# A hybrid HGRN2 and retention layer: one tree for two heads and two blocks, and 512-column retention q/k products

## The chip, the cores and the metric

The kernel runs on one core of a Trainium2 chip. The metric is the device time of one execution in microseconds (us). The engines are named as the profile names them: PE (TensorE matmuls) and PEld (its weight loads), DVE (VectorE), ACT (ScalarE), POOL (GpSimd) and SP (SyncE, which here only issues DMAs; SPq is its queue of issues). Each engine takes its own instructions in a fixed order; an instruction that waits holds up all that stand behind it on that engine.

## The reference

One layer over 2048 positions with model width 1024 and 8 heads of each of two mixers:

```python
h    = rms_norm(x, norm_g) * (1.0 + scale) + shift
proj = h @ w_in
(hq, hf, hi, hz, rq, rk, rv, rz, ga, gb) = split(proj)
oA = hgrn2_chunkwise(hq, hf, hi, lower_bounds)     # S_t = diag(f_t) S_{t-1} + (1-f_t) i_t^T
uA = head_rms_norm(oA, hg_norm_g) * silu(hz)
qB, kB = rotary(rq, pos), rotary(rk, pos)
oB = retention_chunkwise(qB, kB, rv)               # chunks of 128, zeta/xi decays
uB = head_rms_norm(oB, ret_norm_g) * silu(rz)
m  = sigmoid(ga) * uA + sigmoid(gb) * uB
x  = x + gate * (m @ w_out)
out = rms_norm(x, final_g)
```

The HGRN2 heads have 128 channels for q, f and v, the retention heads 64 for q and k and 128 for v. All is float32; dense products are made as three float32r products of a high and a low part.

## The kernel before, in words

**Tiling.** The sequence is cut into two superblocks (sb) of 1024 tokens, each of 8 chunks of 128 or two blocks of 512. In a superblock four pairs of heads (p = 0 to 3) follow one another. For a pair, PE runs four dense stages: **a** (forget gate and q of HGRN2, `gf` and `gq`, four groups for each block), **c** (the v of both mixers, `gv`, one group a chunk), **b** (retention's q and k, `gr`, one group of 256 columns a chunk) and **d** (the gates of the two heads, `gg`, 8 chunks for each head). A group is 8 steps over the contraction (kt = 0 to 7) of three matmuls each (`mm3`), so 24 matmuls. All dense matmuls are recorded under L53.

**Weights.** `Ring` (L447) brings them in the order of use. SP loads a raw tile of two steps (`wa`, `wb`, `wc`, `wd`, L465/L467; two raw tiles exist, NRAW), ACT copies the high part of a step (L482), DVE subtracts for the low part (L483), and the split step sits in one of 9 slots. A slot is freed in the last group of a stage, step by step; a raw tile is free when both its steps are split.

**Background.** Between dense matmuls stand bursts of small ones. `Background.tick` counts dense steps (1 tick is one step of 512 columns) and after GAP = 8 ticks lets every lane give out its next piece: `tree` (seven levels of products `lv` for the HGRN2 scores inside a chunk, one tree for each block and pair of heads, two of them side by side), `retention` (`rt`, then `por`) and `hgrn_out` (`poh`, with the running state `st`). After level 64 a tree transposes k into f on DVE (L666) and posts `place`, 16 DMAs `k<-f` on SP (L673), after which `hgrn_out` may read k by tokens. `rotate` makes the rotary parts on DVE (L760 to L769), transposes them (L772) and posts `send`, four DMAs `qkT<-tr` to DRAM (L777). `fetch` in `retention` makes `kpad` with the decay zeta on DVE (L796) and posts three DMAs from DRAM (L805, L806) into `qpad` and `kT`. A post comes out a given number of ticks later.

**Order.** PE's order is that of the program. All DMAs stand in one queue, SP's. On SP, DVE, ACT and POOL the order is set by the scheduler of the compiler framework and fixed before the run. DVE's `v`, `st`, `qk`, `qs`, `tr`, `wl..` in the profile are the tiles named above.

Of the kernel before, what the change touches and what calls it, by code (L numbers as in the profile page):

```python
# [9 lines left out]
F32 = mybir.dt.float32  # L10
# [12 lines left out]
P = 128  # L23
# [12 lines left out]
NQK = 6  # L36
NGA = 6
GAP = 8.0
# [4 lines left out]
def tile_hybrid(ctx: ExitStack, tc: tile.TileContext, a: dict, out: bass.AP):  # L43
# [47 lines left out]
    def late_consts():  # L91
        m32 = upool.tile([P, 512], I32, name="m32", tag="sg", bufs=3)
        nc.sync.dma_start(out=m32[:, 0:66], in_=a["msk"])
        G.tensor_copy(
            out=msk, in_=m32[:, 0:64].rearrange("p (l t) -> p l t", l=4).unsqueeze(2).broadcast_to([P, 4, 8, 16])
        )
        G.tensor_copy(out=dmsk, in_=m32[:, 64:66].unsqueeze(1).broadcast_to([P, 8, 2]))
        for t, src in lates:
            nc.sync.dma_start(out=t, in_=src)
# [50 lines left out]
    def ada_row_of_c():  # L150

        scb = hpool.tile([P, D], F32, name="scb", tag="h1", bufs=8)
        for i in range(2):
            dg = upool.tile([P, 1025], F32, name=f"dg{i}", tag="k", bufs=2)[:, 0:512]
            for k4 in range(4):
                kt = 4 * i + k4
                V.tensor_scalar(
                    out=dg[:, k4 * P : (k4 + 1) * P], in0=ident, scalar1=sc[:, kt : kt + 1], scalar2=None, op0=ALU.mult
                )
            ps = dense_ps(f"scp{i}")  # L160
            PE.matmul(out=ps, lhsT=ones, rhs=dg, start=True, stop=True)
            V.tensor_copy(out=scb[:, i * 512 : (i + 1) * 512], in_=ps)
# [13 lines left out]
    def ada_row(j):  # L176

        acc = upool.tile([P, 1025], F32, name=f"acc{j}", tag="k", bufs=2)[:, 0:512]
        bg_ = upool.tile([P, 1024], F32, name=f"gate{j}", tag="q", bufs=2)[:, 0:512]
# [20 lines left out]
    msk = cpool.tile([P, 4, 8, 16], U8, name="msk", tag="msk")  # L200
    dmsk = cpool.tile([P, 8, 2], U8, name="dmsk", tag="dmsk")
# [4 lines left out]
    afs, ads = [], []  # L206
    for i in range(2):
        t = cpool.tile([P, 8, P], F32, name=f"af{i}", tag=f"af{i}")
        G.memset(t, 0.0)
        afs.append(t)  # L210
        t = cpool.tile([P, 8, 32], F32, name=f"ad{i}", tag=f"ad{i}")
        G.memset(t, 0.0)
        ads.append(t)
# [122 lines left out]
    def load_x2(t, nm, tag):  # L336
        xt = upool.tile([P, {"q": 1024, "f": 1026}[tag]], F32, name=f"{nm}{t}", tag=tag, bufs=2)[:, 0:1024]
# [50 lines left out]
    def block_r(b):  # L388

        while held.get("f", 0) > 1:  # L390
            yield True
        take("f", 2)
        rb = upool.tile([P, 2, 513], F32, name=f"rb{b}", tag="f", bufs=2)[:, 0, 0:512]
        for t in range(4):
            xt = upool.tile([P, 1024], F32, name=f"xt{b}_{t}", tag="xr", bufs=1)
            nc.sync.dma_start(out=xt, in_=a["x"][(4 * b + t) * P : (4 * b + t + 1) * P, :])
            yield
            yield
            r = x_rstd(t, [xt[:, 0:512], xt[:, 512:1024]], f"b{b}_{t}")
# [9 lines left out]
    def block_h(b):  # L409
# [9 lines left out]
        for kt in range(KT):  # L419
# [8 lines left out]
            else:  # L428
                if kt == KT - 1:
                    give("f")  # L430
# [4 lines left out]
    for sb in range(NSB):  # L435
        for p in range(NP):
            if sb == 0 and p == 0:
                wseq += [(("c", sb, p), a["w_c"][p], 512), (("a", sb, p), a["w_a"][p], 512)]
            else:
                wseq += [(("a", sb, p), a["w_a"][p], 512), (("c", sb, p), a["w_c"][p], 512)]  # L440
            wseq.append((("b", sb, p), a["w_b"][p], 256))
            wseq.append((("d", sb, 2 * p), a["w_d"][2 * p], 512))
            wseq.append((("d", sb, 2 * p + 1), a["w_d"][2 * p + 1], 512))


    slots = [(g, k, 512 // wseq[g][2]) for g in range(len(wseq)) for k in range(0, KT, 512 // wseq[g][2])]

    class Ring:
        def __init__(self):
            self.pairs = [(g, k2) for g in range(len(wseq)) for k2 in range(KT // 2)]  # L450
            self.raw_of = {gk: i for i, gk in enumerate(self.pairs)}
# [7 lines left out]
        def load(self, upto):  # L459
            while self.nraw < min(upto, len(self.pairs)):  # L460
                g, k2 = self.pairs[self.nraw]
                key, src, n = wseq[g]
                w = wpool.tile([P, 2, 512], F32, name=f"w{key[0]}{g}_{k2}", tag="raw", bufs=NRAW)
                if n == 512:
                    nc.sync.dma_start(out=w, in_=src[k2])  # L465
                else:
                    nc.sync.dma_start(out=w[:, 0, :].rearrange("p (k n) -> p k n", k=2), in_=src[k2])  # L467
# [3 lines left out]
        def pump(self, limit=RING):  # L471
            while self.nsplit < min(self.nfree + limit, len(slots)):
                i = self.nsplit
                g, k, two = slots[i]
                key, src, n = wseq[g]
                r = self.raw_of[g, k // 2]
                self.load(r + 1)
                w = self.raws[r].rearrange("p k n -> p (k n)")
                w = w[:, 0:512] if two == 2 else w[:, k % 2 * 512 : k % 2 * 512 + 512]
# [4 lines left out]
                for j in range(two):  # L484
                    self.tiles[key, k + j] = (hi[:, j * n : (j + 1) * n], lo[:, j * n : (j + 1) * n])
                self.nsplit += 1
                done = r + (two == 2 or k % 2 == 1)
                self.load(done + self.ahead)
# [12 lines left out]
    def group_tok(sb, key, cs, n, nm):  # L501

        pss = [dense_ps(f"{nm}_{sb * CH + c}") for c in cs]
        tok_steps(sb, key, cs, n, pss, range(KT))
        return pss

    def tok_steps(sb, key, cs, n, pss, kts):
        for kt in kts:
            ws = ring.tiles[key, kt]
            for c, ps in zip(cs, pss):  # L510
                hh = hts[sb * NBLK + c // 4, kt]
                t = c % 4
                done = mm3(
                    ps[:, 0:n],
                    (hh[0][:, t * P : (t + 1) * P], hh[1][:, t * P : (t + 1) * P]),
                    (ws[0][:, 0:n], ws[1][:, 0:n]),
                    kt == 0,
                    kt == KT - 1,
                )
            if cs[-1] == CH - 1 and (n == 512 or kt % 2):  # L520
                ring.release()
            bg.tick(n / 512 * len(cs))
        return done
# [19 lines left out]
    us = {}  # L543

# [5 lines left out]
    def unit_f(h, b, psf, f, k):  # L550
        j = h % 2
        sg = upool.tile([P, 512], F32, name=f"sgf{h}_{b}", tag="sg", bufs=3)
        S.activation(out=sg, in_=psf, func=AF.Sigmoid)
        if j == 0:
            V.memset(f[:, :, 512:513], 1.0)
        V.tensor_scalar(
            out=f[:, j, 0:512], in0=sg, scalar1=omlb[:, h : h + 1], scalar2=lb[:, h : h + 1], op0=ALU.mult, op1=ALU.add
        )
        V.tensor_scalar(
            out=k[:, j * 512 : (j + 1) * 512], in0=f[:, j, 0:512], scalar1=-1.0, scalar2=1.0, op0=ALU.mult, op1=ALU.add  # L560
        )

    def unit_q(h, b, psq, q):
        j = h % 2
        sg = upool.tile([P, 512], F32, name=f"sgq{h}_{b}", tag="sg", bufs=3)
        S.activation(out=sg, in_=psq, func=AF.Sigmoid)
        V.tensor_tensor(out=q[:, j * 512 : (j + 1) * 512], in0=psq, in1=sg, op=ALU.mult)

    level = {}

    def level_ps(i):

        if level.get("burst") != bg.bursts:
            level["burst"] = bg.bursts
            level["ps"] = small_ps(f"lv{bg.bursts}", "lv")
        return level["ps"][:, i * 256 : (i + 1) * 256]

    def tree(p, b, f, k, q):
        nm = f"{p}_{b}"
        af, ad = afs[b % 2], ads[b % 2]  # L580
        f0 = upool.tile([P, 2], F32, name=f"f0{nm}", tag="f0", bufs=4)
        V.tensor_copy(out=f0, in_=f[:, :, 0])
        kk = k[:, 0:1024]
        k16, q16 = (z.rearrange("p (n t) -> p n t", t=16) for z in (kk, q))
        k16j = kk.rearrange("p (j n t) -> p j n t", j=2, t=16)
        qk0 = upool.tile([P, 64], F32, name=f"qk0{nm}", tag="qk0", bufs=1)
# [6 lines left out]
        for li in range(7):  # L593
            m = 1 << li
            yield
            ps = level_ps(b % 2)
            qm, km = (z.rearrange("p (n two m) -> p n two m", two=2, m=m) for z in (q, kk))
            if m < 16:
                for c in range(8):
# [9 lines left out]
            else:  # L609
                nr = 64 // m  # L610
                for n in range(8 * nr):
# [6 lines left out]
            if m == 1:  # L618
                for u in range(4):
                    PE.matmul(  # L620
                        out=ps[32 * u : 32 * u + 32, 128:144], lhsT=ones[:, 0:32],
                        rhs=qk0.rearrange("p (c u w) -> p c u w", u=4, w=2)[:, :, u, :], start=True, stop=True,
                    )
            yield "mid"
            t_cur = f[:, :, 1:513] if m == 1 else f[:, :, 0 : 2 * nb]
            tv = t_cur.rearrange("p j (n two) -> p j n two", two=2)
            qv = q.rearrange("p (j n two m) -> p j n two m", j=2, two=2, m=m)[:, :, :, 1, :]
            kv = kk if m >= 16 else k[:, 1:1025]
            kv = kv.rearrange("p (j n two m) -> p j n two m", j=2, two=2, m=m)[:, :, :, 0, :]
            V.tensor_tensor(out=qv, in0=qv, in1=tv[:, :, :, 0:1].broadcast_to([P, 2, nb, m]), op=ALU.mult)  # L630
            V.tensor_tensor(out=kv, in0=kv, in1=tv[:, :, :, 1:2].broadcast_to([P, 2, nb, m]), op=ALU.mult)
# [4 lines left out]
            if m == 1:  # L636
                V.copy_predicated(
                    out=ad.rearrange("p c (w j) -> p c w j", w=2)[:, :, :, 0], mask=dmsk,
                    data=ps[:, 128:144].rearrange("p (c w) -> p c w", w=2),
                )  # L640
            if m < 16:
# [3 lines left out]
                    data=ps[:, 0:128].rearrange("p (n m) -> p n m", m=m),  # L645
                )
            elif m == 64:
                for u in range(2):
                    S.activation(
                        out=af[0:64, u : 8 : 2, 64:P],  # L650
                        in_=ps[64 * u : 64 * u + 64, 0:256].rearrange("p (c t) -> p c t", c=4), func=AF.Copy,
                    )
            else:
                for r0 in range(0, P, 2 * m):
                    S.activation(
                        out=af[r0 : r0 + m, :, r0 + m : r0 + 2 * m],
                        in_=ps[r0 : r0 + m, 0 : 8 * m].rearrange("p (c t) -> p c t", c=8), func=AF.Copy,
# [5 lines left out]
        tl = upool.tile([P, 8], F32, name=f"tl{nm}", tag="tl", bufs=4)  # L663
# [569 lines left out]
```

## Time and profile before

| what | number |
|---|---|
| median of three runs | 2119.55 us (2117.77 to 2121.07) |
| the profiled execution | 2116.81 us |
| its span in the trace | 2114.9 us |
| mean granted clock of PE | 0.996 |
| DVE, ACT, POOL busy | 54%, 28%, 6% |
| DMA | 171.05 MB, mean 81 GB/s |

The span runs from the first to the last instruction of the trace; 1.9 us of the profiled execution lie around it. In the chain of waits, and in groups of instructions, the first number of a row is the start or the total in us; in the timeline it is the start, then how long the row lasts, and in brackets how long the engine was idle before it and what it waited for.

### The profile page before, as it was taken

Reading aid. Unit: us, or ns where it says so; the run is one execution under the profiler, and the core shown is the slowest. Engines: PE = TensorE matmul, PEld = TensorE weight load, DVE = VectorE, ACT = ScalarE, POOL = GpSimd, SP = SyncE. Lnnn points to the kernel's source line nnn. Section 1 sums busy time; section 2 is a strip of 40 time slices with the busy share of each in tenths; the row PEclk is TensorE's granted clock in tenths of the full one; section 3 lists DMA queues with packets and bytes.
Section 4 is the critical chain, followed back from the end, with each engine's and each line's share of the span. In section 5 each row is a group of like instructions: output and inputs, shape, how many; then the busy total and the mean of one; then the engine's idle time right before and its main releaser. Section 6 shows DMA issues by size and latency. Waiting matters only on the chain.

```text
span 2114.9 us, 40661 instructions
## 1 busy us (share of the span) xinstructions
PE 2068.9 (98%) x16152; PEld 1747.7 (83%) x16152; DVE 1144.2 (54%) x2977; ACT 589.6 (28%) x1485; POOL 135.9 (6%) x276
## 2 busy tenths in 40 slices
PE   6998999999999999999999999999999999999998
PEld 4887888988888888987888888988888888877886
DVE  7385535654555444657655444653545545566553
ACT  6222213222222223234222223222222223223221
POOL 1001100110001000121001000110001000100000
PEclk9999999999999999999999999999999999999999
DMA  8132211422132211435132211421132212336541
GB/s 321 36 78 50 62 45 47 107 64 53 37 75 58 59 60 45 101 105 157 36 76 57 59 62 45 95 63 49 40 80 52 72 58 61 85 105 210 175 134 60
DMA packets 298365, 171.05 MB, mean 81 GB/s; under 512 B 222912, under 2 KB 259264, under 8 KB 298176
## 3 DMA queue, kind: packets, MB, share of 16 engines
q1 hardware_dynamic: 298176, 168.47, 28.6%
q8 instruction: 127, 2.08, 0.4%
q14 instruction: 62, 0.51, 0.1%
HBM read 134.81 MB, written 25.17 MB: 76 GB/s over the span
## 4 chain that ended last, share of the span: by engine, by line
PE 89%; DVE 4%; DMA 3%; SPq 2%; issue 1%; ACT 0%; POOL 0%; DVEq 0%; POOLq 0%; ACTq 0%
PE gg L53 32%; PE gv L53 15%; PE gq L53 8%; PE gf L53 8%; PE ops L53 8%; PE gr L53 5%; PE por L53 4%; PE lv L53 3%; PE poh L53 3%; PE rt L53 1%; SPq L777 1%; SPq L673 1%; DVE wa L169 1%; DMA wd<-in_w_d_dram 1%; DMA kT<-qkT 1%
## 5 line engine op out<-in xcount | busy, mean ns | idle before, releaser
L53 PE MATMUL gg<-whd,h 128*128 128x512 f32 x2048 | 656.8, 394 | 0.0
L53 PEld LDWEIGHTS gg<-whd,h 128*128 128x128 f32 x2048 | 385.9, 188 | 78.2 <-issue 0.5
L53 PE MATMUL gg<-wld,h 128*128 128x512 f32 x1024 | 399.8, 390 | 0.0
L53 PE MATMUL gv<-whc,h 128*128 128x512 f32 x1024 | 335.4, 399 | 0.0
L53 PEld LDWEIGHTS gv<-whc,h 128*128 128x128 f32 x1024 | 192.6, 189 | 42.0 <-DVE h L363 0.8
L53 PEld LDWEIGHTS gg<-wld,h 128*128 128x128 f32 x1024 | 193.2, 189 | 37.8 <-issue 0.5
L53 PE MATMUL gv<-wlc,h 128*128 128x512 f32 x512 | 199.1, 391 | 1.1 <-DVE wlc L483 1.1
L53 PE MATMUL gr<-whb,h 128*128 128x256 f32 x1024 | 192.2, 285 | 0.0
L855 ACT ACTIVATE sgg<-gg 128x512 f32<-128x512 f32 x128 | 76.1, 595 | 336.2 <-PE gg L53 329.2
L53 PEld LDWEIGHTS gr<-whb,h 128*128 128x128 f32 x1024 | 161.9, 191 | 0.4
L630 DVE TENSOR_TENSOR q<-q,f 128x512 f32<-128x512 f32 x112 | 77.1, 688 | 157.4 <-PE lv L53 157.1
L53 PE MATMUL gf<-h,wha 128*128 128x512 f32 x512 | 159.0, 392 | 1.4 <-ACT wha L482 1.3
L53 PE MATMUL gq<-h,wha 128*128 128x512 f32 x512 | 160.0, 394 | 0.0
L53 PE MATMUL ops<-wo,mh 128*128 128x512 f32 x512 | 157.7, 389 | 0.0
L858 DVE TENSOR_TENSOR ga<-gg,sgg 128x256 f32<-128x256 f32 x128 | 53.8, 420 | 180.5 <-ACT sgg L855 173.4
L53 PE MATMUL gr<-wlb,h 128*128 128x256 f32 x512 | 144.8, 283 | 0.0
L53 PEld LDWEIGHTS gv<-wlc,h 128*128 128x128 f32 x512 | 96.7, 189 | 20.1 <-DVE wlc L483 1.5
L53 PEld LDWEIGHTS gf<-h,wha 128*128 128x128 f32 x512 | 95.3, 188 | 21.6 <-ACT wha L482 2.2
L53 PEld LDWEIGHTS ops<-wo,mh 128*128 128x128 f32 x512 | 96.1, 188 | 19.9
L53 PEld LDWEIGHTS gq<-h,wha 128*128 128x128 f32 x512 | 94.8, 188 | 19.4
L53 PE MATMUL gf<-h,wla 128*128 128x512 f32 x256 | 100.3, 392 | 0.0
L53 PE MATMUL gq<-h,wla 128*128 128x512 f32 x256 | 99.9, 390 | 0.0
(157 smaller groups left out, 2924.8 us busy)
## 6 DMA issues: line engine op xcount, KB each, us to landing
wd<-in_w_d_dram SPq DMA_DIRECT2D x64, 512.0 KB, 3.8
wc<-in_w_c_dram SPq DMA_DIRECT2D x32, 512.0 KB, 3.4
wa<-in_w_a_dram SPq DMA_DIRECT2D x32, 512.0 KB, 3.6
wa<-in_w_ada_dram SPq DMA_DIRECT2D x16, 512.0 KB, 8.4
wb<-in_w_b_dram SPq DMA_DIRECT2D x32, 256.0 KB, 2.6
qkT<-tr SPq DMA_DIRECT2D x256, 32.0 KB, 1.7
k<-f SPq DMA_DIRECT2D x256, 32.0 KB, 2.0
mT_dram<-ga SPq DMA_DIRECT2D x512, 16.0 KB, 1.5
```

The source lines that it names most:

```text
L53: made = nc.tensor.matmul(**kw)
L169: V.tensor_tensor_reduce(out=w, in0=w, in1=scb, scale=1.0, scalar=bad[:, i * KT + kt : i * KT + kt + 1], op0=ALU.mult, op1=ALU.add, accum_ ...
L630: V.tensor_tensor(out=qv, in0=qv, in1=tv[:, :, :, 0:1].broadcast_to([P, 2, nb, m]), op=ALU.mult)
L673: nc.sync.dma_start(out=placed[32 * j : 32 * j + 32, :, i, :], in_=turned[32 * i : 32 * i + 32, :, j, :])
L777: nc.sync.dma_start(out=dm[:, 32 * i : 32 * i + 32].rearrange("(j a) t -> a j t", a=32), in_=tr[32 * i : 32 * i + 32].rearrange("a (j t) - ...
L855: S.activation(out=sg, in_=ps, func=AF.Sigmoid)
L858: V.tensor_tensor(out=ga, in0=ps[:, 0:256], in1=sg[:, 0:256], op=ALU.mult)
```

## The change

One tree now takes both heads and both blocks of a superblock: its f, k and q tiles are twice as large and exist once, its DVE operations are half as many and twice as long, and a pair has 7 bursts of `lv`. Its two `place` posts (one for each block) come 5 and 7 ticks after level 64. The b stage runs for even pairs alone, with 512 columns: q and k of this pair and the next. `rotate` works on 512 columns, also multiplies k by zeta (`kz`) and sends both to DRAM; `fetch` then loads five pieces and makes nothing on DVE. `qk`, `tr` and `kz` have two buffers. Retention and `hgrn_out` start one group earlier, and GAP is 9.

```diff
-NQK = 6
-GAP = 8.0
+GAP = 9.0
...
             if p % 2 == 0:
+                wseq.append((("b", sb, p), a["w_b"][p : p + 2]))
...
+                if key[0] == "b":
+                    for j in range(2):
+                        nc.sync.dma_start(out=w[:, :, j * 256 : (j + 1) * 256], in_=src[j, k2])
+                else:
                     nc.sync.dma_start(out=w, in_=src[k2])
...
-    def tree(p, b, f, k, q):
+    def tree(p, sb, f, k, q):
+        NC = 4 * NU
...
-                for c in range(8):
+                for c in range(NC):
...
-        V.transpose(out=ff, in_=kk)
-        def place():
-            for i in range(4):
-                for j in range(4):
-                    nc.sync.dma_start(out=placed[32 * j : 32 * j + 32, :, i, :], in_=turned[32 * i : 32 * i + 32, :, j, :])
-            give("f")
-            sent.append(True)
         sent = []
-        bg.post(5.0, place)
-        while not sent:
-            yield True
-        yield
-        us[p, b] = (q, kk, af, tl, f0)
+        for bb in range(NBLK):
+            V.transpose(out=ff[:, bb * 1024 : (bb + 1) * 1024], in_=kk[:, bb * 1024 : (bb + 1) * 1024])
+            def place(bb=bb):
+                cs = slice(8 * bb, 8 * bb + 8)
+                for i in range(4):
+                    for j in range(4):
+                        nc.sync.dma_start(
+                            out=placed[32 * j : 32 * j + 32, cs, i, :], in_=turned[32 * i : 32 * i + 32, cs, j, :]
+                        )
+                if bb == NBLK - 1:
+                    give("f")
+                sent.append(bb)
+            bg.post(5.0 + 2.0 * bb, place)
...
     def rotate(p, gc, ps):
-        take("qk", NQK)
-        qk = upool.tile([P, 256], F32, name=f"qk{nm}", tag="qk", bufs=NQK)
+        qk = upool.tile([P, 512], F32, name=f"qk{nm}", tag="qk", bufs=2)
...
-        tr = upool.tile([P, 256], F32, name=f"tr{nm}", tag="tr", bufs=2)
+        tr = upool.tile([P, 512], F32, name=f"tr{nm}", tag="tr", bufs=2)
         V.transpose(out=tr, in_=qk)
+        kz = upool.tile([P, 256], F32, name=f"kz{nm}", tag="kz", bufs=2)
+        V.tensor_tensor(out=kz.rearrange(...), in0=qk.rearrange(...)[:, :, 1], in1=zeta[...], op=ALU.mult)
...
-            turned_qk[p, gc] = (qk, dm)
-        bg.post(3.0, send)
+            nc.sync.dma_start(out=dz, in_=kz)
+            for w in range(2):
+                turned_qk[p + w, gc] = (dm[256 * w : 256 * w + 256], dz[:, P * w : P * w + P])
+        bg.post(4.0, send)
...
         def fetch(n):
-            for j in range(2):
-                V.tensor_scalar(out=kz[:, j * 192 : j * 192 + 64], in0=qk[...], scalar1=zeta[...], op0=ALU.mult)
-            give("qk")
             def load():
                 for j in range(2):
                     r = slice(64 * j, 64 * j + 64)
                     nc.sync.dma_start(out=qT[r, j * P : (j + 1) * P], in_=dm[r])
+                    nc.sync.dma_start(out=kz[:, j * 192 : j * 192 + 64], in_=dz[:, j * 64 : j * 64 + 64])
                 nc.sync.dma_start(out=kTs[n], in_=dm[P : 2 * P])
...
+        if p % 2 == 0:
+            for c in range(CH):
+                if c == CH - 1:
+                    start_lanes()
+                rotate(p, sb * CH + c, group_tok(sb, ("b", sb, p), c, f"gr{p}"))
```

The next rows show where the change puts instructions on three engines. In each, a row is the line, the operation, what it writes and reads, the shape, and how often it stands there in succession; the number after a tile's name tells tiles of one name apart.

First SP's queue in the b stage of pair 2 of the first superblock, before:

```order
L465 DMA wd_0_6363<-in_w_d_dram 128x1024
L673 DMA k_1_5495<-f_1_5494 32x8x32 x2
L465 DMA wd_1_6372<-in_w_d_dram 128x1024
L673 DMA k_1_5495<-f_1_5494 32x8x32
L465 DMA wd_2_6388<-in_w_d_dram 128x1024
L673 DMA k_1_5495<-f_1_5494 32x8x32 x13
L465 DMA wd_3_6420<-in_w_d_dram 128x1024
L777 DMA qkT_0_6486<-tr_0_6484 32x8x32 x4
L777 DMA qkT_1_6524<-tr_1_6522 32x8x32 x4
```

and now, at the same place:

```order
L456 DMA wd_1_5899<-in_w_d_dram 128x1024
L643 DMA k_0_4970<-f_0_4969 32x8x32 x32
L761 DMA qkT_0_5987<-tr_0_5983 32x16x32 x4
L765 DMA kz_0_5988<-kz_0_5985 128x256
L761 DMA qkT_1_6045<-tr_1_6041 32x16x32 x4
...
L765 DMA kz_4_6172<-kz_4_6169 128x256
L761 DMA qkT_5_6213<-tr_5_6209 32x16x32 x4
L765 DMA kz_5_6214<-kz_5_6211 128x256
L456 DMA wd_2_6271<-in_w_d_dram 128x1024
```

The loads of weights for the gates stood between the DMAs of `place`; `wd_2` (steps 4 and 5 of the first head's gates) now stands behind 32 of them and behind the sends of chunks 0 to 5.

Next DVE at the end of that b stage, now: `wld_6301` is the low part of step 3 of the gates, `st` the HGRN2 state, and `tr_5` what the send of chunk 5 reads.

```order
L469 TENSOR_TENSOR wld_6301<-wd_1_5899,whd_6300 128x512
L713 SCALAR_TENSOR_TENSOR st_129<-st_129,tl_0_5942,poh_1_6375 128x128
L748 STREAM_TRANSPOSE tr_4_6167<-qk_4_6161 128x512
L750 TENSOR_TENSOR kz_4_6169<-qk_4_6161,zeta 128x256
L713 SCALAR_TENSOR_TENSOR st_130<-st_130,tl_0_5942,poh_1_6375 128x128
L736 TENSOR_TENSOR qk_6_6245<-gr_6_6215,cos_1067 128x512
L736 TENSOR_TENSOR qs_6_6246<-gr_6_6215,sin_1069 128x512
L666 SCALAR_TENSOR_TENSOR v_1_5380<-poh_1_6375,rrh_1_6385,gn_2_0_6257 128x128
L744 TENSOR_TENSOR qk_6_6245<-qk_6_6245,qs_6_6246 128x8x32
L745 TENSOR_TENSOR qk_6_6245<-qk_6_6245,qs_6_6246 128x8x32
L666 SCALAR_TENSOR_TENSOR v_1_5380<-poh_1_6375,rrh_1_6385,gn_2_0_6257 128x128
L748 STREAM_TRANSPOSE tr_5_6209<-qk_5_6203 128x512
```

The state update, which reads PE's `poh_1`, stands ahead of both transposes, so `tr_5` comes after `poh_1`. On PE, `poh_1` now stands here, in the first group of the gates; `whd_6309` and `wld_6310` are the two parts of step 4, split from `wd_2`:

```order
L52 MATMUL gg_0_6367<-whd_6267,h_1_292 128x512
L52 MATMUL poh_1_6375<-v_1_5380,k_0_4970 128x128
L52 MATMUL poh_1_6375<-v_1_5380,af 128x128
L52 MATMUL poh_1_6375<-st_129,q_0_4971 128x128
L52 MATMUL poh_1_6375<-v_1_5380,k_0_4970 128x128
L52 MATMUL poh_1_6375<-v_1_5380,af 128x128
L52 MATMUL poh_1_6375<-st_130,q_0_4971 128x128
L52 MATMUL gg_0_6367<-whd_6293,h_2_330 128x512
L52 MATMUL gg_0_6367<-wld_6294,h_2_330 128x512
L52 MATMUL gg_0_6367<-whd_6293,h_2_330 128x512
L52 MATMUL gg_0_6367<-whd_6300,h_3_362 128x512
L52 MATMUL gg_0_6367<-wld_6301,h_3_362 128x512
```

One more matmul of step 3 follows, and then those of step 4. The even pairs of the second superblock have the same order, with `poh_8` in the place of `poh_1`.

Last SP in pair 1 of the second superblock, an odd pair, which has no b stage, now:

```order
L787 DMA kT_11_13202<-qkT_11_10833 128x128
L643 DMA k_1_12080<-f_1_12079 32x8x32 x32
L785 DMA qpad_113<-qkT_11_10833 64x128
L786 DMA kpad_119<-kz_11_10834 128x64
L785 DMA qpad_113<-qkT_11_10833 64x128
L786 DMA kpad_119<-kz_11_10834 128x64
L859 DMA mT_dram<-ga_8_13107 32x4x32 x4
```

The 32 DMAs of both blocks stand in one piece, with retention's fetches of chunk 11 behind them; before, a block's 16 stood by themselves. In pair 3 of this superblock it reads the same; in the odd pairs of the first superblock the 32 follow on `kT_3`, and `poh_0` waits for their first half; in the first pair of all they stand between the fetches of chunks 1 and 2.

305 lines of the change are left out of this document (145 added, 160 removed).

## Prediction

> **What bounds the kernel now.** I read the page's busy times first, then the chain of waits.
>
> ```profile
> PE 2068.9 (98%) x16152; PEld 1747.7 (83%) x16152; DVE 1144.2 (54%) x2977; ACT 589.6 (28%) x1485; POOL 135.9 (6%) x276
> PE 89%; DVE 4%; DMA 3%; SPq 2%; issue 1%; ACT 0%; POOL 0%; DVEq 0%; POOLq 0%; ACTq 0%
> PE gg L53 32%; PE gv L53 15%; PE gq L53 8%; PE gf L53 8%; PE ops L53 8%; PE gr L53 5%; PE por L53 4%; PE lv L53 3%; PE poh L53 3%; PE rt L53 1%; SPq L777 1%; SPq L673 1%; DVE wa L169 1%; DMA wd<-in_w_d_dram 1%; DMA kT<-qkT 1%
> ```
>
> PE sets the end: it is busy for 98% of the span, and 89% of the chain is PE, mostly dense groups. A change gains only by shortening what PE does, or the few waits it has, and loses by every new wait on PE. DVE (54%) has room on the whole, so its halved instruction count is worth nothing by itself. Now the waits that PE has:
>
> ```profile
> PE rt L53 <- DMA kT<-qkT: 8.0, 8, 2.0
> 168.64 0.80 PE L53 MATMUL poh<-v,k 128*128 128x128 f32 x2 [5.56 <-DMA k<-f]
> 164.00:168.60 4.60, 0.00 (x0) 0.00 (x0) 1.84 (x5) 0.63 (x3) 0.00 (x0) 0.92 0.25 41
> 168.60:172.00 3.40, 3.36 (x12) 3.07 (x13) 0.55 (x3) 0.62 (x3) 0.00 (x0) 0.50 0.97 212
> 172.00:174.80 2.80, 2.80 (x8) 2.15 (x8) 1.41 (x5) 0.23 (x2) 0.89 (x2) 0.51 0.29 65
> 174.80:180.00 5.20, 5.20 (x41) 4.47 (x41) 1.74 (x7) 0.60 (x1) 0.00 (x0) 1.00 0.18 39
> ```
>
> The first row is of the waits (total, times, longest), the second of the timeline, the others of windows, where the number ahead of the last two is the granted clock. In all 8.0 us go at `rt`, and 5.56 us once at `poh`, in the first pair, where the 16 place DMAs land late. That wait has a tail: the clock is 0.50 to 0.51 for 3.4 + 2.8 = 6.2 us after it, so half of that, 3.1 us, is lost too. A shorter wait has no tail:
>
> ```profile
> 867.96 0.67 PE L53 MATMUL rt<-qpad,kT 128*128 128x256 f32 x2 [1.97 <-DMA kT<-qkT]
> 868.00:872.00 4.00, 4.00 (x33) 3.95 (x34) 2.01 (x8) 0.09 (x1) 0.00 (x0) 1.00 0.37 57
> ```
>
> After 1.97 us idle the clock is 1.00. So I charge 3.1 us after waits near or above 5.56 us, none near 2, and half, 1.6, for 4 to 5 us between them. The Trainium skill, "TensorE: Matmul & The Clock Gate", section "What's actually happening", says that the clock halves after an idle window of about 3.4 us and comes back after a busy one. The trace agrees in kind, but its slow stretch is 6.2 us and not 3.4; by the page a tail would cost 1.7 us as an estimate, and the sum below would be some 10 us lower.
>
> **What the change saves.**
>
> ```profile
> 1093.57 5.75 PE gr L53 x48
> 1221.25 5.44 PE gf L53 x24
> ```
>
> In the chain, 48 matmuls of 256 columns take 5.75 us, so a `gr` group of 24 takes 2.875; a group of 512 takes 5.44. The 64 groups of before cost 184.0, the 32 of now 174.1: **9.9 us saved**.
>
> ```profile
> 779.61 0.39 PE L53 MATMUL gf<-h,wla 128*128 128x512 f32 x1
> 779.93 0.74 PE L53 MATMUL lv<-q,k 128*32 128x16 f32 x64
> 780.59 0.73 PE L53 MATMUL gf<-h,wha 128*128 128x512 f32 x2
> 781.16 0.40 PE L53 MATMUL gf<-h,wla 128*128 128x512 f32 x1
> ```
>
> A dense matmul starts 5.44/24 = 0.227 us after another. Here `lv` starts 0.32 after the last one (0.09 late), and behind the burst two dense matmuls take 0.57 in place of 0.45 (0.12 late): a burst costs 0.2 us beside its own matmuls, whose number does not change. The stretches of small matmuls fall from 202 to 166 in PE's order (those with `lv` from 88 to 56), so 36 x 0.2: **7.2 us saved**.
>
> If none of before's waits came back, 8.0 + 5.6 + 3.1 = 16.7 us would go as well; I take them all out and then put in what comes in their place. That leaves 2116.8 - 9.9 - 7.2 - 16.7 = 2083.0.
>
> **What the change adds: waits behind SP's queue.**
>
> ```profile
> 155.63 11.65 SPq L673 DMA_DIRECT2D k<-f  x16
> 860.60 3.88 SPq L777 DMA_DIRECT2D qkT<-tr  x8
> 859.95 0.55 SPq L465 DMA_DIRECT2D wd<-in_w_d_dram  x1
> wd<-in_w_d_dram SPq DMA_DIRECT2D x64, 512.0 KB, 3.8
> k<-f SPq DMA_DIRECT2D x256, 32.0 KB, 2.0
> qkT<-tr SPq DMA_DIRECT2D x256, 32.0 KB, 1.7
> ```
>
> SP needs 11.65/16 = 0.73 us to issue a place DMA, 0.485 for a send, 0.55 for a weight load, which lands 3.8 us later. The 32 place DMAs in one piece hold SP for 23.3 us.
>
> *Even pairs after the first (three).* All of it in rows of the front part: `wd_2` stands behind the send of chunk 5, that behind `tr_5`, and DVE comes to `tr_5` only after `st`, which waits for `poh_1`, six matmuls into the first gate group. From the start of `poh_1` PE has its own six matmuls (about 0.9 us) and six dense ones (6 x 0.227), so 2.3 us, until it wants step 4 of the weights. Nothing else stands in PE's order that could cover more. The other side:
>
> ```profile
> L630 DVE TENSOR_TENSOR q<-q,f 128x512 f32<-128x512 f32 x112 | 77.1, 688 | 157.4 <-PE lv L53 157.1
> L772 DVE STREAM_TRANSPOSE tr<-qk 128x256 f32<-128x256 f32 x64 | 27.6, 435 | 20.1 <-DMA qkT<-tr 19.9
> L760 DVE TENSOR_TENSOR qk<-gr,cos 128x256 f32<-128x256 f32 x64 | 26.7, 416 | 3.2 <-PE gr L53 3.2
> L768 DVE TENSOR_TENSOR qk<-qk,qs 128x128 f32<-128x128 f32 x64 | 18.2, 285 | 1.1
> L739 DVE SCALAR_TENSOR_TENSOR st<-st,tl,poh 128x128 f32<-128x128 f32 x112 | 35.5, 335 | 2.5 <-PE poh L53 2.4
> L693 DVE SCALAR_TENSOR_TENSOR v<-poh,rrh,gn 128x128 f32<-128x128 f32 x128 | 39.3, 347 | 95.9 <-POOL rrh L116 95.7
> L482 ACT ACTIVATE whd<-wd 128x512 fp32r<-128x512 f32 x128 | 76.3, 626 | 49.7 <-DMA wd<-in_w_d_dram 43.6 <-PE gr L53 2.5 <-PE gg L53 1.4
> L483 DVE TENSOR_TENSOR wld<-wd,whd 128x512 fp32r<-128x512 f32 x128 | 84.1, 682 | 14.6 <-ACT whd L482 14.5
> ```
>
> First half of `poh_1` 0.45. Then on DVE, in the order shown: two `st` 0.67, two `tr` of 512 columns at 0.8 (between the 0.435 of 256 and its double), `kz_4` 0.42 (the row of 256 columns at L760), `qk_6` and `qs_6` 0.69 each (the row of 512 columns), two `v` 0.69, and the two halves of the rotation 0.42 each (0.285 for half the columns), 5.6 in all. On SP four sends and `kz_5`, 5 x 0.485 = 2.4, and `wd_2` 0.5. It lands 3.8 later, ACT takes 0.63 and DVE 0.69. Sum 0.45 + 5.6 + 2.4 + 0.5 + 3.8 + 1.3 = 14.0, less 2.3: **PE waits 11.7 us**, with 3.1 for the clock 14.8 a pair, 44.4 for three. Below it is bounded by 8: no DVE work but `st`, `tr` and `kz` (about 2), as if the rest had been done. Above by 22: a send now moves twice as many pieces, and if its issue takes twice 0.485, SP comes out of the 32 place DMAs with six sends of 4.4 in place of 2.4, up to 10 us later at `wd_2`. I take the row's own 0.485, since place and send have equally many pieces each and yet differ by half, so pieces alone do not set it. The Trainium skill, "DMA: Bandwidth & Descriptors", section "Anatomy of one DMA", says of another path of issue that many descriptors can be emitted before their cost shows; no row here has this shape.
>
> *Odd pairs (four).* A block's tree ends with a transpose:
>
> ```profile
> L666 DVE STREAM_TRANSPOSE f<-k 128x1024 f32<-128x1024 f32 x16 | 19.9, 1242 | 0.3
> ```
>
> From the start of level 64 to the first place DMA I count 7 us: 0.7 for the burst, 2 x 1.37 for DVE's last two products (twice the 0.688 of 512 columns), 1.24 for the first transpose, and some 2.3, an estimate, for the DVE work of other lanes between them. In the first superblock 16 place DMAs follow and their landing, 7 + 11.7 + 1.4 = 20.1 (1.36 is what lay between the end of the issue at 167.28 and `poh` at 168.64). PE wants `poh_0` 19 ticks of 0.68 and 2.5 us of small matmuls after level 64, at 15.4. In the second, retention's fetch stands behind all 32: 7 + 23.3 + 2 for its own issues + 2.0 to land = 34.3, against some 30 for `rt`. Either gives 4 to 5 us, **4.4 and half a tail of 1.6, 24 us for four**. Bounds: 0 a pair, if level 64 ends on DVE as early as the ticks allow, and 8.7 (the 5.56 of before with its tail).
>
> *The first pair.* It waited 5.6 + 3.1 before; now `poh_0` waits again, and the fetch of chunk 2 stands behind 32 place DMAs rather than 16. I take **13**, between 8.7, as before, and 8.7 + 11.65 - 3.1 = 17 if the second half of the DMAs is exposed to `rt` with the tail already paid.
>
> Two fetch DMAs more a chunk, and four weight loads halved into two, cost SP time and nothing on PE: they lie behind gate groups, where SP idles. DVE loses 128 `kpad` operations and gains 32 `kz`, both beside PE. GAP changes where bursts stand, which the count of stretches holds.
>
> **Sum.** 2083.0 + 44.4 + 24 + 13 = **2164 us**, against 2116.8 of the profiled execution, which is itself 2.7 under the median of 2119.55.
>
> **The rivals.**
>
> *SP keeps its lead* (faster). The place is `wd_2` in SP's queue. It decides from the point where the send of chunk 5 leaves SP 3.3 us before PE starts `poh_1`, 11.7 earlier than I walk: issue, landing and split then take 5.6 us against 3.3 + 2.3, and the same lead has the place DMAs out in time. PE then keeps only the wait of the first pair: 2083.0 + 8.7 = **2092**. For it: before, such loads stood between place DMAs, and PE's idle time ahead of the gate groups was 0.0:
>
> ```profile
> L53 PE MATMUL gg<-whd,h 128*128 128x512 f32 x2048 | 656.8, 394 | 0.0
> ```
>
> Against: DVE's order, where `st` stands before `tr_5`; no speed of SP mends that. Chance 0.24.
>
> *Only the place waits come* (`wd_2` in time, the odd pairs and the first as above): 2083.0 + 24 + 13 = **2120**. Against it the same rows speak. Chance 0.12.
>
> *Sends cost by the piece.* Ten us more in each of three even pairs: **2194**. For it: twice the pieces. Against: the unequal prices of equal pieces. Chance 0.16.
>
> My forecast has 0.48.
>
> **How the numbers follow.** A measurement of this kernel can tell about 0.2%, 4 us. Slower by more: the forecast, the last rival, and a quarter of the second, 0.67. Within: some half of the second, 0.07. Faster: the first rival and the rest, 0.26. The range reaches from the middle of the first rival to that of the last, 2092 to 2195, which leaves out half of each, 0.12 and 0.08; the forecast's own, from its bounds, is 2145 to 2185.
>
> **What would show it.** In the trace after: `gr` rows at 0.227 a matmul; 56 `lv` bursts; in three even pairs a wait of 9 to 14 us in the first gate group, put down to `whd` or `wld`, with the clock near 0.5 after it; waits of 4 to 5 us of `poh` or `rt` for `k<-f` or `kT` in the odd pairs. Sends issued at 0.97 would speak for the last rival. If PE waits less than 30 us in all, I am wrong about the order in which DVE frees SP.

## The result and the profile after

The changed kernel takes 2155.1 us (median of 4 runs, 2153.07 to 2156.91) against 2120.31 of the kernel before on the same chip: a ratio of 1.0164, 95% interval 1.0147 to 1.0182. It is slower. The profiled execution has a span of 2154.2 us, 39.3 more than the 2114.9 of before.

First the page of the changed kernel, in the three parts that were shown of before:

```profile
PE 2062.0 (96%) x15320; PEld 1713.1 (80%) x15320; DVE 1096.0 (51%) x2441; ACT 570.4 (26%) x1389; POOL 141.7 (7%) x274
PE 79%; SPq 6%; DVE 6%; DMA 5%; issue 2%; ACT 1%; POOL 1%; DVEq 0%; POOLq 0%; ACTq 0%
PE gg L52 27%; PE gv L52 14%; PE gq L52 8%; PE ops L52 8%; PE gf L52 8%; SPq L643 6%; PE poh L52 3%; PE por L52 3%; PE lv L52 2%; PE gr L52 2%; DMA wd<-in_w_d_dram 2%; PE rt L52 1%; DVE wa L169 1%; DVE wld L469 1%; DMA wb<-in_w_b_dram 1%
```

PE is busy for 7 us less than before, although some of that time runs at half clock. In the chain PE fell from 89% to 79%, and the place DMAs (SPq L643) rose from 1% to 6%: the end now hangs in part on SP's queue. Where, the waits of PE in the timeline tell (start, duration, then in brackets the idle time ahead and what ended it):

```profile
184.87 1.19 PE L52 MATMUL rt<-qpad,kT 128*128 128x256 f32 x2 [5.97 <-DMA kT<-qkT]
216.45 1.19 PE L52 MATMUL rt<-qpad,kT 128*128 128x256 f32 x2 [7.17 <-DMA kT<-qkT]
423.70 0.46 PE L52 MATMUL poh<-v,k 128*128 128x128 f32 x2 [3.70 <-DMA k<-f]
677.89 0.79 PE L52 MATMUL gg<-whd,h 128*128 128x512 f32 x1 [11.36 <-ACT whd L468]
906.36 0.77 PE L52 MATMUL poh<-v,k 128*128 128x128 f32 x2 [4.84 <-DMA k<-f]
1170.38 0.80 PE L52 MATMUL gg<-whd,h 128*128 128x512 f32 x1 [11.71 <-ACT whd L468]
1648.31 0.79 PE L52 MATMUL gg<-whd,h 128*128 128x512 f32 x1 [12.12 <-ACT whd L468]
1889.35 0.67 PE L52 MATMUL rt<-qpad,kT 128*128 128x256 f32 x2 [1.24 <-DMA qpad<-qkT]
```

Three waits of 11.4 to 12.1 us stand in the first gate group of the three even pairs after the first; two of 3.7 and 4.8 in the odd pairs of the first superblock; two of 6.0 and 7.2 in the first pair. All waits of PE above 0.4 us after the first 60 us, added up from the brackets of the timeline, are 67.6 us, and 20.2 before. I use this sum below for every kernel.

The first of the three can be followed in the timelines of SP, then DVE:

```profile
627.06 22.31 SPq L643 DMA_DIRECT2D k<-f  x32
...
659.21 1.94 SPq L761 DMA_DIRECT2D qkT<-tr  x4
661.24 0.46 SPq L765 DMA_DIRECT2D kz<-kz  x1
666.19 1.93 SPq L761 DMA_DIRECT2D qkT<-tr  x4
668.23 0.45 SPq L765 DMA_DIRECT2D kz<-kz  x1
670.63 1.93 SPq L761 DMA_DIRECT2D qkT<-tr  x4
672.66 0.45 SPq L765 DMA_DIRECT2D kz<-kz  x1
673.21 0.88 SPq L456 DMA_DIRECT2D wd<-in_w_d_dram  x2
```

```profile
665.20 0.35 DVE L713 SCALAR_TENSOR_TENSOR st<-st,tl,poh 128x128 f32<-128x128 f32 x1 [1.93 <-PE poh L52]
665.46 0.70 DVE L748 STREAM_TRANSPOSE tr<-qk 128x512 f32<-128x512 f32 x1
...
669.90 0.70 DVE L748 STREAM_TRANSPOSE tr<-qk 128x512 f32<-128x512 f32 x1
...
677.87 2.66 DVE L469 TENSOR_TENSOR wld<-wd,whd 128x512 fp32r<-128x512 f32 x4 [2.67 <-ACT whd L468]
```

DVE waits 1.93 us for `poh_1`, updates the state, and makes `tr_4` and, 4.4 us later, `tr_5`. SP, which was idle from 661.70 to 666.19, issues each send when its transpose is done, and `wd_2` at 673.21. PE had run out at 666.5, and goes on at 677.89. The clock after it, in windows (the number ahead of the last two):

```profile
677.80:680.00 2.20, 2.11 (x4) 1.45 (x5) 2.06 (x4) 1.71 (x4) 0.00 (x0) 0.50 1.09 205
680.00:682.00 2.00, 2.00 (x6) 1.55 (x5) 0.53 (x1) 0.00 (x0) 0.00 (x0) 0.50 0.90 240
682.00:684.00 2.00, 2.00 (x6) 1.52 (x6) 0.00 (x0) 0.29 (x1) 0.00 (x0) 0.51 0.48 128
684.00:686.00 2.00, 2.00 (x11) 1.63 (x10) 1.45 (x3) 0.83 (x2) 0.00 (x0) 1.00 0.82 166
```

The clock comes back at 683.94. So 6.05 us run at half clock, 3.0 are lost, as after the wait of before.

### The profile page after: what moved, and what is told of

Same layout as the page of the kernel before. It is cut to its first block, busy times and chain, and to the rows that moved or that the text cites. A ratio compares the mean times of both kernels' runs of the same rounds, so it can differ in the third digit from the quotient of the medians.

```text
span 2154.2 us, 38274 instructions
## 1 busy us (share of the span) xinstructions
PE 2062.0 (96%) x15320; PEld 1713.1 (80%) x15320; DVE 1096.0 (51%) x2441; ACT 570.4 (26%) x1389; POOL 141.7 (7%) x274
## 4 chain that ended last, share of the span: by engine, by line
PE 79%; SPq 6%; DVE 6%; DMA 5%; issue 2%; ACT 1%; POOL 1%; DVEq 0%; POOLq 0%; ACTq 0%
PE gg L52 27%; PE gv L52 14%; PE gq L52 8%; PE ops L52 8%; PE gf L52 8%; SPq L643 6%; PE poh L52 3%; PE por L52 3%; PE lv L52 2%; PE gr L52 2%; DMA wd<-in_w_d_dram 2%; PE rt L52 1%; DVE wa L169 1%; DVE wld L469 1%; DMA wb<-in_w_b_dram 1%
## 5 line engine op out<-in xcount | busy, mean ns | idle before, releaser
L52 PE MATMUL gg<-whd,h 128*128 128x512 f32 x2048 | 671.9, 400 | 35.5 <-ACT whd L468 35.2
L52 PEld LDWEIGHTS gg<-whd,h 128*128 128x128 f32 x2048 | 390.9, 191 | 117.7 <-ACT whd L468 36.4
L52 PE MATMUL gr<-whb,h 128*128 128x512 f32 x512 | 162.0, 392 | 2.3 <-DVE qs L736 2.3
L468 ACT ACTIVATE whd<-wd 128x512 fp32r<-128x512 f32 x128 | 77.7, 627 | 207.8 <-PE gr L52 109.1
L597 DVE TENSOR_TENSOR q<-q,f 128x1024 f32<-128x1024 f32 x56 | 68.5, 1223 | 110.3 <-PE lv L52 110.3
L469 DVE TENSOR_TENSOR wld<-wd,whd 128x512 fp32r<-128x512 f32 x128 | 85.0, 687 | 59.3 <-ACT whd L468 58.6
L52 PEld LDWEIGHTS gr<-whb,h 128*128 128x128 f32 x512 | 96.1, 188 | 23.5 <-PE gr L52 3.4
L115 POOL TENSOR_TENSOR rrr<-ssr,mhalf 128x2 f32<-128x2 f32 x64 | 44.7, 698 | 1038.8 <-DVE ssr L114 1038.8
L663 ACT ACTIVATE jkr<-por 128x128 f32<-128x128 f32 x128 | 35.5, 278 | 260.4 <-DVE rs L823 216.5
```

What stands on the lines that cost most here:

```text
L52: made = nc.tensor.matmul(**kw)
L115: G.tensor_tensor(out=dst, in0=ss, in1=mhalf.broadcast_to([P, width]), op=ALU.pow)
L468: S.activation(out=hi, in_=w, func=AF.Copy)
L469: V.tensor_tensor(out=lo, in0=w, in1=hi, op=ALU.subtract)
L663: S.activation(out=junk, in_=po[:, i * P : (i + 1) * P], func=AF.Square, accum_out=ss[:, i : i + 1])
```

## The experiments

Theory A is that of the prediction: `wd_2` is held by SP's order (it stands behind the send of chunk 5) and that send by DVE's order (the state update ahead of `tr_5`). The rivals are told in the expectations. The edits are on the changed kernel except where another is named.

**hgrn_late.**

```diff
-            bg.lanes.append(hgrn_out(p, sb * NBLK, vs, gns[0]))
+            later.append(hgrn_out(p, sb * NBLK, vs, gns[0]))
+            if p % 2:
+                bg.lanes.append(later.pop())
...
+                if j == 0 and c == 2 and later:
+                    bg.lanes.append(later.pop())
                 ps = group_tok(sb, ("d", sb, h), c, f"gg{h}")
```

> Edit: in even pairs the HGRN2 output lane starts two gate groups later, so that no state update stands ahead of the transposes tr_4 and tr_5 on DVE; the order of SP is the same, and so is the rest of DVE's. Theory A (wd_2 is held by DVE's order: state update waits for poh_1, then tr_5, then the send of chunk 5): DVE is freed some 6 us earlier there, and PE, which no longer has poh_0 and poh_1 ahead of the place, arrives 2.2 us earlier, so the waits in the three first gate groups fall from 11.4 to 12.1 us to about 7.7. Rival B (SP's backlog behind 32 place DMAs alone sets when wd_2 is issued): the issue does not move, and the waits grow to about 14.

Measured: 2164.7 us in its one timed run, span 2162.9. PE's waits can't be read as either theory had it, since the burst that `poh_1` left was taken by retention's first product:

```profile
679.49 1.19 PE L52 MATMUL rt<-qpad,kT 128*128 128x256 f32 x2 [15.61 <-DMA kT<-qkT]
```

What can be read is when SP issues `wd_2`, in its timeline:

```profile
665.93 1.93 SPq L761 DMA_DIRECT2D qkT<-tr  x4
667.96 0.45 SPq L765 DMA_DIRECT2D kz<-kz  x1
668.51 0.88 SPq L456 DMA_DIRECT2D wd<-in_w_d_dram  x2
```

Level 64 starts at 618.14 here and at 617.85 in the changed kernel, so `wd_2` comes 50.4 us after it, not 55.4. The state update on DVE holds `wd_2` by 5.0 us, near the 6 expected; the step's weights are split at 673.9, still some 8 us after PE would have wanted them with nothing in `poh_1`'s place. So DVE's update is 5 of the 11.4 us and not all of it. What holds `wd_2` now is still DVE: SP sends chunks 4 and 5 at 662.88 and 665.93, each as soon as its transpose is done.

```profile
653.13 0.71 DVE L748 STREAM_TRANSPOSE tr<-qk 128x512 f32<-128x512 f32 x1 [2.45 <-DMA qkT<-tr]
662.15 0.70 DVE L748 STREAM_TRANSPOSE tr<-qk 128x512 f32<-128x512 f32 x1
665.20 0.71 DVE L748 STREAM_TRANSPOSE tr<-qk 128x512 f32<-128x512 f32 x1
```

And DVE is late because its transpose at 653.13 waited for the send of chunk 0 (`tr` has two buffers), which stood behind the place DMAs on SP.

**memset_late.**

```diff
-            V.memset(f[:, :, 512:513], 1.0)
+            V.tensor_scalar(
+                out=f[:, :, 512], in0=sg[:, 0:NU], scalar1=0.0, scalar2=1.0, op0=ALU.mult, op1=ALU.add
+            )
```

> Edit: the write of ones into the pad column of f is tied to the sigmoid of the next pair, so that it no longer stands on DVE in the middle of the b stage, where DVE was idle for 9.7 us ahead of it until all place DMAs had landed. Theory A: nothing changes at the first gate groups (waits of 11 to 12 us), since the transpose behind it waits for the send of chunk 0, which stands behind the same place DMAs on SP. Rival C (the memset holds DVE, and so the sends): the three waits fall by up to 9.7 us each, the time by up to 30 us.

Measured: span 2154.2 us, the same, with waits of 11.40, 11.66 and 12.09 us in the three places (one timed run, 2156.0). Rival C falls. An idle time of 9.7 us on DVE cost nothing, because what stood behind it waited for the same queue.

**send_act.**

```diff
-                nc.sync.dma_start(
+                nc.scalar.dma_start(
                     out=dm[:, 32 * i : 32 * i + 32].rearrange("(j a) t -> a j t", a=32),
...
-            nc.sync.dma_start(out=dz, in_=kz)
+            nc.scalar.dma_start(out=dz, in_=kz)
```

> Edit: the sends of qkT and kz to DRAM are issued by ACT's queue instead of SP's. Theories A and B: wd_2 no longer stands behind sends, and the three waits in the first gate group (35.2 us with some 8 us of half clock after them) fall below 2 us each: the time falls to about 2112 us, by some 3 to 6 more if the first pair gains too. Rival D (the free raw tiles and slots set when wd_2 can be issued): waits of 5 us and more stay, and the time stays above 2135.

Measured: 2117.8 us (median of 10), ratio to before 0.9982 (0.9971 to 0.9993): the 1.6% are back with one queue changed. The waits for `whd` are gone; in their place stand 2.80, 2.78 and 2.60 us, more than the 2 that I allowed, put down to the split on DVE:

```profile
657.36 0.50 PE L52 MATMUL gg<-wld,h 128*128 128x512 f32 x1 [2.80 <-DVE wld L469]
```

ACT's timeline shows why:

```profile
649.75 2.89 ACTq L761 DMA_DIRECT2D qkT<-tr  x4
652.74 0.46 ACTq L765 DMA_DIRECT2D kz<-kz  x1
653.24 0.63 ACT L468 ACTIVATE whd<-wd 128x512 fp32r<-128x512 f32 x1 [38.63 <-DMA qkT<-tr]
```

The split of step 1 now stands on ACT behind the sends, as the load stood on SP. Rival D (tiles and slots) falls; the sum of PE's waits is 28.8 us.

**poh_hold.**

```diff
             while bb not in sent:
                 yield True
+            t0 = bg.now
+            while p % 2 and bb == 0 and bg.now < t0 + 9.0:
+                yield True
             yield
```

> Edit: in odd pairs the HGRN2 output lane waits 9 ticks more after its place DMAs have been posted. Theory A (in the odd pairs of the first superblock poh_0 comes a few us before the place DMAs have landed): the waits of 3.7 and 4.8 us with the half clock after them go, some 10 us: 2145. Rival E (another wait takes their place, retention or the next group finds the same queue): the sum of PE's waits in these pairs stays above 6 us and the time within 4 us of 2155.

Measured: 2151.5 us in its one timed run, span 2149.7, 4.5 less. Both waits of `poh` (8.5 us) are gone, but the sum of waits falls by 4.0 only, to 63.6: there is now 1.74 and 2.51 at `rt` in the second superblock where it was 0 and 1.24, 2.16 in place of 1.10 at the first `gf`, and the first pair waits 1.3 longer. The time stays within 4 us of 2155, as E has it, and the waits left at `rt` (4.3 us) are under the 6 of E: between A and E.

**place_act.**

```diff
+                        q_of = nc.scalar if bb and p % 2 == 0 else nc.sync
-                        nc.sync.dma_start(
+                        q_of.dma_start(
```

> Edit: in even pairs the 16 place DMAs of the second block are issued by ACT's queue, so SP is held 11 us less before the sends. On DVE the state update still stands ahead of tr_5, though tr_4 and five other operations now stand ahead of it. Theory A (from poh_1 to the split weights it is one chain through DVE): the chain is 3.8 us shorter on DVE, so the waits in the three first gate groups fall from 11.4 to 12.1 us to about 7.5 and no further. Rival B (SP's backlog behind place): wd_2 is issued 11 us earlier, and the waits are below 2 us.

Measured: 2141.5 us in its one timed run. The waits are 9.88, 9.83 and 10.20 us, 1.5 to 1.9 less each and not below 2: rival B falls as the whole cause, and the 7.5 of A is missed as well. The sum of PE's waits falls by 12.4 us, to 55.2; only 5.3 of these lie in the three places. SP had 11 us more, and spent them waiting:

```profile
644.52 1.93 SPq L762 DMA_DIRECT2D qkT<-tr  x4
646.57 0.43 SPq L766 DMA_DIRECT2D kz<-kz  x1
659.37 2.02 SPq L762 DMA_DIRECT2D qkT<-tr  x4
```

From 647.00 to 659.37 SP stands at the send of chunk 4, whose transpose is at 658.64 on DVE, behind three splits of gate weights that wait for slots that PE frees in the last `gr` group. My 7.5 counted the chain from `poh_1`, but not these splits. So freeing SP of half the place DMAs leaves about 10 us, and freeing DVE of the update alone would leave some 8 (from hgrn_late, worked out and not seen as a wait): the load stands behind both, and taking it from behind the sends, in send_act, removed both.

**gr_only**, on the kernel before: the parts of the change in `Ring`, `rotate`, `fetch` and the b stage alone (with `xt` in halves, as in the changed kernel).

```diff
+            if p % 2 == 0:
+                wseq.append((("b", sb, p), a["w_b"][p : p + 2]))
...
-        qk = upool.tile([P, 256], F32, name=f"qk{nm}", tag="qk", bufs=NQK)
+        qk = upool.tile([P, 512], F32, name=f"qk{nm}", tag="qk", bufs=2)
```

> Edit: the kernel before with the 512-column q/k products, kz through DRAM and five fetch DMAs alone; the trees stay as they were, one for each block. Theory A: the products save 9.9 us, but wd_2 stands behind the send of chunk 5 here too (and behind a fetch), so waits of 8 us and more come in the first gate groups of the three even pairs, and with the clock it is 2120 - 10 + 30 or more: about 2140. Rival F (the waits come only where one tree posts 32 place DMAs at once): below 2115.

Measured: 2147.1 us (4 runs), ratio 1.0126 (1.0111 to 1.0141). The time is near what I expected, the way is not: PE waits at most 0.8 us in the gate groups. The waits are 44.6 us in all, and the longest are those of retention and of the first pair:

```profile
168.10 0.77 PE L53 MATMUL poh<-v,k 128*128 128x128 f32 x2 [6.01 <-DMA k<-f]
217.88 1.19 PE L53 MATMUL rt<-qpad,kT 128*128 128x256 f32 x2 [10.45 <-DMA kT<-qkT]
693.83 1.19 PE L53 MATMUL rt<-qpad,kT 128*128 128x256 f32 x2 [5.38 <-DMA kT<-qkT]
```

SP is done with the place DMAs of pair 2 and at retention's fetches by 639.5, and `wd_2` is issued at 670.81, 6.3 us before the first gate group, and comes in time. So the sends ahead of `wd_2` do not make the wait by themselves.

Rival F had that part right, but its time, below 2115, is missed. What else the wait needs is not separated, because this run also leaves out a third part of the change. The section on the change says that retention and `hgrn_out` start one group earlier; that holds for the odd pairs. In the even pairs they start ahead of the last `gr` group, and before (and here) ahead of the first: the first `poh` of pair 2 comes at 656.60 in the changed kernel and at 620.33 here. With this later start `poh_1` came to stand in the first gate group. Whether the wait comes from it or from the one tree was not tried.

What is late here is `kT`, whose fetch shares the queue with the sends and the weights; which of the DMAs ahead of it costs most was not tried.

**tree_only**, on the kernel before: the one tree, its place DMAs and GAP alone (with four buffers of `qk` in place of six, and `xt` in halves, for room in SBUF).

```diff
-    def tree(p, b, f, k, q):
+    def tree(p, sb, f, k, q):
+        NC = 4 * NU
...
+            bg.post(5.0 + 2.0 * bb, place)
```

> Edit: the kernel before with the one tree for two heads and two blocks, its 32 place DMAs together and GAP 9 alone; q/k products of 256 columns for each pair, three fetch DMAs. Theory A: the bursts save 7.2 us, all four weight loads of the first gates stand ahead of the place DMAs on SP, so no wait of a gate group for its weights; retention's first fetch stands behind 29 place DMAs and may wait 3 to 6 us in each of eight pairs: between 2113 and 2145. Rival F: 32 DMAs at once hold the weights here as well, with waits above 8 us for whd.

Measured: 2324.2 us (4 runs), ratio 1.0953 (1.0934 to 1.0971). No gate group waits for `whd`, as A had it (two wait 1.5 us for `wld`), but `rt` waits by far more than my 3 to 6 us:

```profile
679.65 1.19 PE L53 MATMUL rt<-qpad,kT 128*128 128x256 f32 x2 [22.71 <-DMA kT<-qkT]
```

```profile
657.24 18.93 SPq L663 DMA_DIRECT2D k<-f  x29
676.21 1.25 SPq L801 DMA_DIRECT2D qpad<-qkT  x2
677.51 0.58 SPq L802 DMA_DIRECT2D kT<-qkT  x1
```

Seven such waits sum to 160.8 us. A b stage of 256 columns is half as long (23 us by 2.875 a group) and retention starts in it, so its first fetch stands behind all of the place DMAs with nothing to cover them. My error was to take the cover of the 512-column stage for granted. In the changed kernel that stage covers the place DMAs in the even pairs. In the odd pairs q and k were made a pair earlier: the first `kT` of pair 3 is issued at 754.42, its first product is at 887.30. So the one tree loses without the wider products. This run, too, starts retention ahead of the first `gr` group; what a later start alone would give was not tried.

**send_pool_hold.** As poh_hold, and the sends on the third queue:

```diff
-                nc.sync.dma_start(
+                nc.gpsimd.dma_start(
                     out=dm[:, 32 * i : 32 * i + 32].rearrange("(j a) t -> a j t", a=32),
...
-            nc.sync.dma_start(out=dz, in_=kz)
+            nc.gpsimd.dma_start(out=dz, in_=kz)
```

> Edit: as poh_hold, with the sends issued by GpSimd's queue instead of SP's. With the sends on ACT (send_act) ACT took the gates' first split only after the send of chunk 5, and PE still waited 2.8, 2.8 and 2.6 us for it; on GpSimd nothing of the weights stands behind a send. Theory A: those waits and the two of poh_0 (3.9 and 3.8) go, with their half clocks: 2098 to 2106 us. Rival G (GpSimd issues slowly, so that retention's fetches or the norms that it makes come late): waits of rt or por of 3 us and more a pair, and no gain over send_act.

Measured: 2099.9 us (4 runs), ratio 0.9898 (0.9883 to 0.9913). The waits in the gate groups are 0.78 us at most, and there is none of `poh` in the odd pairs. One wait of `rt` is 3.86, the first pair keeps one of 5.67, and the sum is 21.3, about that of before. A holds; of G one wait in one pair is seen. The sends on GpSimd without the hold of poh_hold were not run, so the two parts of this gain are not separated.

**best** and **best_gap8**, on send_pool_hold.

```diff
-            while p % 2 and bb == 0 and bg.now < t0 + 9.0:
+            while (p % 2 or sb + p == 0) and bb == 0 and bg.now < t0 + 9.0:
...
-GAP = 9.0
+GAP = 8.0
```

(the last two lines in best_gap8 alone)

> Edit: as send_pool_hold (sends on GpSimd, the HGRN2 output of odd pairs 9 ticks later), and the same 9 ticks in the first pair, where poh_0 still waited 5.67 us. Theory A: that wait and its half clock go, 5 to 8 us: 2092 to 2096. Rival E (the place DMAs ahead of retention's fetches make another wait in the first pair): no change beyond 2 us.

> Edit: as best, with GAP 8 in place of 9. The number of stretches of small matmuls goes from 148 to 151, worth 0.6 us at 0.2 us each: Theory A (GAP is worth nothing by itself): within 3 us of best. Rival H (the level products come before DVE is done with the level ahead, so PE waits for DVE): waits of lv for DVE of more than 0.5 us and 5 us more in all.

Measured: best 2090.5 us (4 runs), a little under what I expected, ratio 0.9865 (0.9847 to 0.9882), sum of waits 15.2, the first pair has none left above 0.5. best_gap8 2085.2 us (4 runs), ratio 0.9830 (0.9816 to 0.9845), sum of waits 12.2. It is 5.3 faster than best, more than the 3 I allowed. With GAP 8 the waits of `rt` of 1.70 and 3.39 us do not come, and `gr` has two new ones of 1.75 and 1.87; the sum of waits explains 3.0 of the 5.3, and the rest stays open. There is no wait of `lv` for DVE, so H falls. Both are faster than the kernel before and the changed one.

## Why the prediction was right

**The forecast** was 2164 us, slower, by three waits at `wd_2` and some smaller ones; it is 2155.1.

**Even pairs.** Charged at 11.7 us each; 11.36, 11.71 and 12.12 measured. The chain from `poh_1` came out by its steps: DVE took 5.4 us from the state update at 665.20 to the end of `tr_5` at 670.60, against 5.6 charged, then come sends of 1.93 and 0.45, the load and the split. Two errors offset each other: the update starts 1.5 us after `poh_1` (663.66 on PE) and not 0.45, and PE goes on with the high part 0.7 us after its split begins and does not wait the 1.3 for both parts. What the walk did not say is that a second hold stands close behind the update: SP's place DMAs delay the send of chunk 0, that delays DVE's transposes, and these the later sends. Without the update the issue of `wd_2` moved by 5.0 us and not by the whole of the wait (hgrn_late); with half of the place DMAs off SP but the update kept, the wait fell by 1.5 to 1.9 us only (place_act).

**What was wrong in size.** In the *odd pairs* the first superblock waits 3.70 and 4.84 us against 4.4 charged, but the second only 0 and 1.24. There PE's product comes 32.0 us after level 64, not 30, and SP needs 20.94 and 21.89 us for 32 place DMAs, not 23.3: two small errors against a margin of 4 us. That is 7.6 us of waits too many, 10.8 with the tails charged for them, more than the 9 us by which the forecast is high. The *first pair* waits 5.97 + 0.83 + 7.17 = 14.0 us and has 3.7 of tails, against 13 charged with tails; the savings below, some 5 us larger than charged, offset that. So the direction and the three waits were foreseen, and that the sum came within 9 us is in part luck. Not foreseen were 2.2 and 1.4 us of `rb` for GpSimd and 2.3 of `gr` for DVE.

**The tails.** Charged were 3.1 us after the long waits, 1.6 after 4 to 5 us and none near 2. Windows set on the switches of the clock (the number ahead of the last two) show what came, here after waits of 3.70, 11.36 and 2.17 us:

```profile
423.70:424.53 0.83, 0.83 (x7) 0.83 (x8) 0.00 (x0) 0.00 (x0) 0.00 (x0) 1.00 0.28 45
424.53:427.94 3.41, 3.41 (x11) 2.73 (x10) 0.86 (x4) 1.10 (x5) 0.89 (x2) 0.50 0.35 51
670.29:677.89 7.60, 0.00 (x0) 0.00 (x1) 4.63 (x11) 0.68 (x2) 0.00 (x0) 0.50 0.74 187
677.89:683.94 6.05, 6.05 (x14) 4.45 (x15) 2.57 (x4) 1.84 (x4) 0.00 (x0) 0.50 0.84 191
963.83:967.25 3.42, 3.42 (x12) 2.84 (x11) 1.30 (x3) 0.74 (x4) 0.88 (x2) 0.50 0.21 48
```

After 3.70 us idle PE still runs 0.83 us at 1.00 and then 3.41 us at 0.50. Around the wait of 11.36 us the clock is 0.50 from 670.29 to 683.94, 13.65 us or four times 3.41, and 6.05 of these lie behind the wait. Half of the half-clock time behind the seven waits of the first pair, the odd pairs and the even pairs is 2.1, 1.6, 1.7, 1.4, 3.0, 2.5 and 2.5 us, 14.9 in all. An eighth tail of 1.7 us follows the wait of 2.17 us at `rb` that ends at 962.51, so "none near 2" does not hold as a rule; with it the tails are 16.6 us.

The Trainium skill, "TensorE: Matmul & The Clock Gate", section "What's actually happening", says that the clock goes by windows of about 3.4 us that run by themselves and that the kernel does not reset. The trace agrees: the stretches at 0.50 last 3.41, 6.83 (167.89 to 174.72, before) and 13.65 us. A tail measured once, as the 6.2 us of the prediction, is therefore no fixed price of a wait; here 11.4 to 12.1 us idle cost 2.5 to 3.0. By the 1.7 us that the prediction worked out from the page as an estimate, its sum would have been some 6 us lower (1.4 in each of the three even pairs and in the first pair) and not 10.

**The savings.** 17.1 us were charged for fewer, wider products and fewer bursts. The 39.3 us of difference are 47.4 of waits and 13.6 of tails (16.6 less the 3.0 of before) less what was saved: 21.7. best_gap8 gives about the same from the other side: its span of 2082.8 is 32.1 below before, of which 8.0 are waits and 1.3 tails (the 3.0 of before less 1.7 that it has after a wait of 2.44 us at `gf`), so 22.8. The mechanism was right, and the sum some 5 us too small; which of its two terms was too small was not separated.

**The rivals.** *SP keeps its lead* did not come, but it told the price: without the waits it gave 2092, and best has 2090.5. That they come so close is in part luck: 2092 charges 8.7 us of wait and tail where best keeps 15.2 of waits, and it counts the savings some 5 us too small. *Sends cost by the piece* fell: a send of twice the pieces is issued in 1.93 us, 0.48 a DMA, as the 0.485 of before. That agrees with what the Trainium skill, "DMA: Bandwidth & Descriptors", section "Anatomy of one DMA", says of another path: many descriptors before their cost shows.

What was not tried is to take the update off DVE and the place DMAs off SP at once and leave `wd_2` behind the sends.

## What to carry to other kernels

When work is merged into longer pieces, read the issue queue and not only the busy engine: a load that PE needs must not stand behind a DMA whose source is made late. Moving the late-sourced DMAs to another queue alone took back the loss of 1.6% (send_act); with a later HGRN2 output in the odd pairs, and on a queue where no weights stand behind them, they gave a gain of 1.0% (send_pool_hold), and one more hold and GAP 8 made it 1.7%. Freed time on one engine is worth less than its length while a second one holds the same load: 11 us of place DMAs off SP took 1.5 to 1.9 us from each wait. So test the two apart.

## What the runs showed of the hardware

GpSimd takes 0.65 us for each DMA of a send (its timeline in send_pool_hold), where SP takes 0.48 and ACT 0.72 (the rows above; the other sends on ACT from 621 to 650 take 0.59 to 1.11):

```profile
642.64 2.58 POOL L764 DMA_DIRECT2D qkT<-tr  x4 [4.42 <-DVE qk L748]
```

And SP's issue is slower right behind weight loads: after the two `wd` loads at 673.21 in the changed kernel one `kz` takes 1.80 us in place of 0.45 (1.72 in hgrn_late and 1.79 in place_act at the same place). Why is not shown:

```profile
676.64 1.80 SPq L765 DMA_DIRECT2D kz<-kz  x1
```
